# Feature blocks bank by bank at both ends of an output step, x blocks three ahead, two small moves

## The chip, the cores and the metric

The kernel runs on one core of one Trainium2 chip. The metric is device time in microseconds, the median of several runs. The core has five engines that work side by side, each with its own queue of instructions that it runs in order: PE (TensorE, matrix products into PSUM banks), PEld (its weight loads), DVE (VectorE), ACT (ScalarE), POOL (GpSimd), and SP, which here issues nearly all DMAs. They wait for each other by semaphores.

## The reference

One inference step of a decoder layer that mixes two branches. 1024 prompt tokens with 16 learned meta tokens ahead of them, and 8 x 4 sample tokens with a paged cache of 1024 positions, go through a common input projection, a stick-breaking attention branch and a gated linear attention branch, a gate on each, and one output projection:

```
h = rms_norm(x, norm_pre_g)
(q, k, v), sg, (gq, gk, gv, gf), gg = branch_inputs(h, w_in, w_alpha, b_alpha)
o_sb = sb_prompt(q, k, v, sb_bias)            # or sb_sample with the paged cache
o_gla, s_end = gla_prompt(gq, gk, gv, gf)     # or gla_chunk on the sample states
mixed = concatenate([o_sb * silu(sg), rms_norm(o_gla) * silu(gg)])
x = x + rms_norm(mixed @ w_out, norm_post_g)
```

Inside `branch_inputs`, the logarithm of the decay is `log_sigmoid(ga @ w_alpha + b_alpha) / 16`, with `ga` the 16 low-rank columns of the input projection. All is float32. The outputs are y for prompt and samples, the new keys and values, and the new states.

## The kernel before

Every float32 product is three products of a rounded high half and the remaining low half of its operands (high x high, high x low, low x high), so a matmul of the algorithm is three matmuls on PE.

The program is written as a main line of projections with side work woven in. A `Weaver` holds generators; `W.beat()`, called after every few matmuls, lets those that are due issue their next instructions. The order in each engine's queue is then set at build time by a planner that simulates the program: of the instructions that are ready in its simulation it takes the one written first, and those written under `urgent()` ahead of all others. It sets the semaphores too. `add_manual_dep(..., NOSYNC)` only forces an order in a queue.

Three stages matter here.

**Low-rank columns** (`low_rank`, lines 367 to 389). Three PSUM accumulators collect the 32 rows of `ga` (high and low weights) for three chunks of tokens. For each of five pieces ACT writes the rounded value to rows 0 to 31 of the tile `g` (L387) and again to rows 64 to 95 (L388), both from PSUM, and DVE writes the remainder to rows 32 to 63 (L389). The next input projection takes the same accumulators.

**Sample states** (`chunks`, lines 985 to 1053). For each of four GLA heads, after the eight prompt chunks, a loop over the eight samples b multiplies keys by values (L1042) and updates a state (L1044). States come by DMA into five buffers: those of b = 5, 6, 7 are loaded at the end of turns 0, 1, 2 (`load_state`, L993). The query products with the states (L1035) are issued in two groups of four, at b = 0 for states 0 to 3 and at b = 6 for states 4 to 7.

**Output projection** (lines 1288 to 1664). The product mixed @ w_out is done with seven products of half-size blocks, numbered p, in place of eight. Each p has two column halves q, and each (p, q) is a `step`: eight feature blocks k of 128 rows, four PSUM banks t of 128 tokens x 512 columns. For each k, `weights` asks for a 128 x 512 weight block by DMA into one of seven `wr` buffers (L1393), casts it on ACT into the high half (L1394) and subtracts on DVE for the low half (L1395), in a ring of four slots; then `product` issues three matmuls into each of the four banks (L1595 to L1597). The steps p = 1, 2, 3, 7 also have sixteen small sample products (L1615) after k = 3 and after k = 7, which read the raw weight blocks, so a `wr` buffer is free only after them. At the end of a step `take` copies or adds the four banks to SBUF (L1443, L1446, L1453, L1456, L1461, L1465, some urgent). Steps run in pairs (1,2), (6), (5,3), (7,4); the second of a pair adds into the same banks once the first's have been read, and the next pair takes two free banks and the first two of the last pair. The last step, (4, 1), has weights kept in SBUF and runs bank by bank throughout (lines 1656 to 1663).

Beside steps 7 and 4, `finish0` (L1510) finishes the first 512 tokens: sixteen blocks of x are fetched by DMA into the four `fr` buffers (L1519), DVE multiplies the output by its norm and adds x (L1530), and the result is stored (L1531). A fetch is ordered on SP behind the newest weight load that was written by then (`behind_ring`). For the first eight blocks a turn lasts two beats, for the others one.

Of the kernel before, what the change touches and what calls it, by code (L numbers as in the profile page):

```python
# [84 lines left out]
def hybrid_step(ctx: ExitStack, tc: tile.TileContext, x_prompt, x_sample, cache_k, cache_v, state_gla,  # L85
# [281 lines left out]
    def low_rank():  # L367

        acc = [accp.tile([P, 512], F32, tag="acc", name=f"acc_ga_{c}") for c in range(3)]
        for kb in range(0, NK, 4):  # L370
            for c, (lo, hi) in enumerate(CHUNKS):
                n = hi - lo
                for k in range(kb, kb + 4):
                    mm(acc[c][:32, :n], wa[k // 8][:, k % 8, :], hh[k][:, lo:hi], start=(k == 0), stop=False)
                    mm(acc[c][:32, :n], wa[k // 8][:, k % 8, :], hl[k][:, lo:hi], start=False, stop=(k == NK - 1))
                W.beat()
            W.beat()
        while not ga:
            W.beat()
        g = ga[0]  # L380
        for c, (lo, hi) in enumerate(CHUNKS):
            for a, b, d in ((max(lo, META), min(hi, REAL), -META), (lo, META, SEQ), (REAL, hi, 0)):
                if a >= b:
                    continue
                with urgent():
                    ps, cs = acc[c][:32, a - lo:b - lo], slice(a + d, b + d)
                    act.copy(g[0:32, cs], ps)  # L387
                    act.copy(g[64:96, cs], ps)  # L388
                    vec.tensor_tensor(g[32:64, cs], ps, g[0:32, cs].bitcast(F32), ALU.subtract)  # L389

    lvl = {}

# [344 lines left out]
    with tc.tile_pool(name="gp", bufs=1) as gp, tc.tile_pool(name="gps", bufs=1, space=PSUM) as gps:  # L737
# [247 lines left out]
        def chunks(g, at, qt, gv, pv, res):  # L985

            kd, ebl, pk = res["kd"], res["ebl"], res["pk"]
            S = None
            Ss = {}

            def load_state(b):
                Ss[b] = gp.tile([P, DV], F32, tag="Sb", bufs=5, name=f"Sb{g}_{b}")
                nc.sync.dma_start(Ss[b][:], state_gla[0, b, g])  # L993

            U = gps.tile([P, DV], F32, tag="U", name=f"U{g}_m")
            for f in range(2):
                mm(U[:, f * P:(f + 1) * P], kd[:META, 8 * P:9 * P], gv[f][:META, 8 * P:9 * P], start=True, stop=True)
            S = gp.tile([P, DV], F32, tag="S", bufs=2, name=f"S{g}_m")
            act.copy(S[:], U[:])
            yield 2  # L1000
            for c in range(8):
                ow = stage(f"ow{g}_{c}")
                ssq = gp.tile([P, 2], F32, tag="ssq", bufs=3, name=f"gssq{g}_{c}")
                U = gps.tile([P, DV], F32, tag="U", name=f"U{g}_{c}")
                for f in range(2):
                    mm(U[:, f * P:(f + 1) * P], kd[:, c * P:(c + 1) * P], gv[f][:, c * P:(c + 1) * P], start=True, stop=True)
                o = gps.tile([P, DV], F32, tag="o", name=f"o{g}_{c}")
                for f in range(2):
                    oh = o[:, f * P:(f + 1) * P]
                    mm(oh, at[:, slot(c), :], gv[f][:, c * P:(c + 1) * P], start=True, stop=False)  # L1010
                    mm(oh, qt[:, col(c):col(c) + P], S[:, f * P:(f + 1) * P], start=False, stop=True)
                Sn = gp.tile([P, DV], F32, tag="S", bufs=2, name=f"S{g}_{c}")
                vec.scalar_tensor_tensor(Sn[:], S[:], ebl[:, c:c + 1], U[:], ALU.mult, ALU.add)
                S = Sn
                act.copy(ow[:, :DV], o[:])
                act.activation(o[:], ow[:, :DV], AF.Square, accum_out=ssq[:, 0:1])
                W.spawn(chunk_out(g, c, ow, ssq[:, 0:1]), 1)
                if c > 2:
                    load_state(c - 3)
                yield 2  # L1020
            nc.sync.dma_start(new_state_prompt[0, 0, g], S[:])

            os_ = gps.tile([P, 2, DV], F32, tag="o", name=f"os{g}")
            for f in range(2):
                for i in range(2):
                    for j in range(4):
                        b = 4 * i + j
                        mm(os_[32 * j:32 * j + 32, i, f * P:(f + 1) * P], at[:48, 8, 16 + NT * b:48 + NT * b],
                           gv[f][:48, 8 * P:9 * P], start=(f == 0 and i == 0), stop=False, skip_group_check=True)
            for b in range(NB):  # L1030
                if b in (0, 6):
                    for j in range(4):
                        e = b // 6 * 4 + j
                        n = REAL + NT * e
                        mm(os_[32 * j:32 * j + 32, b // 6, :], qt[:, n:n + 32], Ss[e][:], start=False, stop=True,  # L1035
                           skip_group_check=True)
                Sb = Ss[b]
                km = stg.tile([96, 384], F32R, tag="stg", name=f"km{g}_{b}")[:, :P]
                vec.tensor_scalar(km, pk[:].bitcast(F32), rmask[:, b:b + 1], None, ALU.mult)
                yield 2  # L1040
                U = gps.tile([P, DV], F32, tag="U", name=f"Us{g}_{b}")
                mm(U[:], km, pv[:], start=True, stop=True)  # L1042
                sn = stage(f"sn{g}_{b}")[:, :DV]
                vec.scalar_tensor_tensor(sn, Sb[:], ebl[:, 9 + b:10 + b], U[:], ALU.mult, ALU.add)  # L1044
                nc.sync.dma_start(new_state_sample[0, b, g], sn)
                if b + 5 < NB:
                    load_state(b + 5)
            ssq = gp.tile([P, 2], F32, tag="ssq", bufs=3, name=f"gssq{g}_s")
            ow = [stage(f"ow{g}_s{i}")[:, :DV] for i in range(2)]
            for i in range(2):  # L1050
                act.copy(ow[i], os_[:, i, :])
                act.activation(os_[:, i, :], ow[i], AF.Square, accum_out=ssq[:, i:i + 1])
            W.spawn(samples_out(g, ow, ssq), 1)
# [236 lines left out]
    with ExitStack() as out:  # L1290
# [219 lines left out]
        def finish0():  # L1510
            r = scale((0, 1, 2, 3))
            todo = [(i, b) for i in range(4) for b in (0, 1)] + [(i, b) for i in range(4) for b in (2, 3)]
            xs = {}

            def fetch(n):
                if n < len(todo):
                    i, b = todo[n]
                    xs[n] = raw(f"xr{i}_{b}")[:]
                    behind_ring(nc.sync.dma_start(xs[n], x_prompt[0, i * P:(i + 1) * P, b * 512:(b + 1) * 512]).ins)  # L1519

            def load_xr(i, b):
                behind_ring(nc.sync.dma_start(xr[i, b], x_prompt[0, 512 + i * P:512 + (i + 1) * P, b * 512:(b + 1) * 512]).ins)

            fetch(0)
            fetch(1)
            for n, (i, b) in enumerate(todo):
                fetch(n + 2)
                yield 2 if n < 8 else 1
                o = sums_[i, b]
                vec.scalar_tensor_tensor(o, o, r[:, i:i + 1], xs.pop(n), ALU.mult, ALU.add)  # L1530
                nc.sync.dma_start(y_prompt[0, i * P:(i + 1) * P, b * 512:(b + 1) * 512], o)  # L1531
                if n == 7:
                    late_ = [slot(14 + f, f"xrs{f}") for f in range(2)]
                if n >= 8:
                    xr[i, b - 2] = late_[b - 2][:, i * 512:(i + 1) * 512].bitcast(F32)
                    load_xr(i, b - 2)
            for i in range(4):
                for b in (2, 3):
                    xr[i, b] = ytile(f"xr1_{i}_{b}")
                    load_xr(i, b)  # L1540
                    yield 1
# [59 lines left out]
        def step(p, q, banks, first, last):  # L1601
# [2 lines left out]
            if p in (1, 3):  # L1604
                SB[c, q] = ops.tile([P, 512], F32, tag="S", bufs=2, name=f"sc{c}{q}")
            raws = []
            for k in range(8):
                w = weights(p, q, k)
                for t in range(4):
                    product(banks[t], t, p, k, w[:2], first, last)  # L1610
                if c is not None:
                    raws.append(w[2])
                    if k % 4 == 3:
                        for e, j in itertools.product((k - 3, k - 1), range(4)):
                            mm(SB[c, q][32 * j:32 * j + 32, :256], small[SAMPLE[p]][:, e + j // 2, :],  # L1615
                               raws[e % 4 + j // 2][:, j % 2 * 256:j % 2 * 256 + 256], start=p in (1, 3) and e == 0,
                               stop=p in (2, 7) and e == 6, skip_group_check=True)
                        raws = []
                W.beat()
# [74 lines left out]
```

## Time and profile before

| | |
|---|---|
| runs | 2058.46, 2059.08, 2063.94 us |
| median | 2059.08 us |
| the profiled execution's own time | 2062.69 us |
| its span, first to last instruction | 2061.0 us |
| mean granted clock of PE | 0.998 |
| HBM read, written | 241.75 MB, 57.31 MB |
| output projection on PE | from 1718.0 us to 2051.4 us |

The profile is of one execution. Its page gives each engine's busy time; the view of waits says for which engine's instruction, or for which DMA, another stood idle, with total, times and longest. A timeline row has start, duration, engine, line, operation, output and inputs, shape, count, and in brackets the idle time before it and what ended it. Matmuls overlap, so the durations in the rows are longer than the distance from one to the next; the distance is what counts. Names such as `b` (output banks), `ring` (weight halves), `wr` (weight blocks), `q` (quarters of the mixed features), `xr` (x blocks), `u`, `y`, `c` (output sums) are those of the program.

### The profile page before, as it was taken

What the parts mean: (1) busy time and instruction counts of PE and PEld (TensorE: products, weight loads), DVE (VectorE), ACT (ScalarE), POOL (GpSimd) and SP (SyncE); (2) the same over time, 40 slices, a digit from 0 to 9 for tenths busy, and PEclk for the clock granted to TensorE, in tenths of its full rate; (3) what the DMA queues carried; (4) which work ended last, traced back from release to release, by engine and by line L of the source; (5) the groups of instructions that cost most, each with busy time, mean ns of one, the idle gap of its engine ahead of it and who ended that gap; (6) DMA issues with size and microseconds to landing.
All of it is one profiled execution on the core that took longest, in us unless ns stands there. A gap on an engine that the chain in (4) does not pass through costs nothing.

```text
span 2061.0 us, 41982 instructions
## 1 busy us (share of the span) xinstructions
PE 2023.1 (98%) x12507; PEld 1864.4 (90%) x12507; DVE 1551.5 (75%) x6282; ACT 953.5 (46%) x2293; POOL 85.1 (4%) x304
## 2 busy tenths in 40 slices
PE   6999999999999999999999999999999999999998
PEld 5999999999999998999999999999888898788776
DVE  7368989888988989899898888978444347554566
ACT  7355555565655556433534335343433325432332
POOL 0012000101000000000000000000000000000000
PEclk9999999999999999999999999999999999999999
DMA  6344454645455452443433434335776666352475
GB/s 202 104 139 147 140 158 134 169 134 147 146 157 147 141 126 73 138 107 80 108 103 80 126 81 115 93 87 166 241 228 230 222 227 195 134 163 75 148 272 175
DMA packets 371821, 301.85 MB, mean 146 GB/s; under 512 B 42360, under 2 KB 312104, under 8 KB 371592
## 3 DMA queue, kind: packets, MB, share of 16 engines
q1 hardware_dynamic: 371288, 298.64, 48.5%
q8 instruction: 98, 1.61, 0.3%
q14 instruction: 131, 1.07, 0.2%
q10 hardware_dynamic: 304, 0.53, 0.1%
HBM read 241.75 MB, written 57.31 MB: 145 GB/s over the span
## 4 chain that ended last, share of the span: by engine, by line
PE 84%; DVE 7%; DMA 3%; ACT 3%; issue 2%; SPq 1%; POOL 0%; DVEq 0%; ACTq 0%; POOLq 0%
PE acc_g L342 5%; PE acc_g L343 5%; PE acc_g L344 5%; PE b L1595 4%; PE b L1597 4%; PE b L1596 4%; PE acc_gv L342 3%; PE acc_gv L343 3%; PE acc_gv L344 3%; PE acc_k L342 3%; PE acc_k L344 3%; PE acc_k L343 3%; PE acc_v L342 2%; PE acc_v L344 2%; PE acc_v L343 2%; PE acc_q L342 2%
## 5 line engine op out<-in xcount | busy, mean ns | idle before, releaser
L464 DVE SCALAR_TENSOR_TENSOR jk<-kp,qb 128x128 f32<-128x128 f32 x2048 | 592.9, 289 | 43.2 <-DMA qb<-qsd 1.5
L342 PE MATMUL acc_g<-hT,wh_g 128*128 128x368 f32 (+2 forms) x768 | 251.1, 327 | 0.5 <-DVE ga L389 0.5
L343 PE MATMUL acc_g<-hT,wh_g 128*128 128x368 f32 (+2 forms) x768 | 247.2, 322 | 0.0
L344 PE MATMUL acc_g<-hT,wl_g 128*128 128x368 f32 (+2 forms) x768 | 246.8, 321 | 0.0
L1595 PE MATMUL b<-ring,f 128*128 128x512 f32 x416 | 164.7, 396 | 4.7 <-DVE u L1465 2.1
L464 DVE DVE_READ_ACCUMULATOR jk<-kp,qb 128x1 f32 x2048 | 166.7, 81 | 0.0
L1596 PE MATMUL b<-ring,f 128*128 128x512 f32 x416 | 163.3, 392 | 0.2 <-DVE ring L1395 0.2
L1597 PE MATMUL b<-ring,f 128*128 128x512 f32 x416 | 162.5, 391 | 0.0
L342 PEld LDWEIGHTS acc_g<-hT,wh_g 128*128 128x128 f32 x768 | 144.3, 188 | 13.1 <-issue 11.2
L1395 DVE TENSOR_TENSOR ring<-wr,ring 128x512 fp32r<-128x512 f32 x104 | 71.3, 689 | 102.4 <-ACT ring L1394 100.2
L343 PEld LDWEIGHTS acc_g<-hT,wh_g 128*128 128x128 f32 x768 | 144.4, 188 | 0.7
L344 PEld LDWEIGHTS acc_g<-hT,wl_g 128*128 128x128 f32 x768 | 144.2, 188 | 0.0
L1394 ACT CAST ring<-wr 128x512 fp32r<-128x512 f32 x104 | 64.2, 620 | 143.4 <-PE b L1597 83.7
L342 PE MATMUL acc_gv<-hT,wh_gv 128*128 128x400 f32 (+2 forms) x384 | 130.3, 339 | 0.0
L342 PE MATMUL acc_k<-hT,wh_k 128*128 128x384 f32 (+1 forms) x384 | 126.3, 329 | 0.0
L343 PE MATMUL acc_gv<-hT,wh_gv 128*128 128x400 f32 (+2 forms) x384 | 125.2, 326 | 0.0
L342 PE MATMUL acc_q<-hT,wh_q 128*128 128x368 f32 (+2 forms) x384 | 124.9, 325 | 0.0
L344 PE MATMUL acc_gv<-hT,wl_gv 128*128 128x400 f32 (+2 forms) x384 | 124.6, 325 | 0.0
L344 PE MATMUL acc_k<-hT,wl_k 128*128 128x384 f32 (+1 forms) x384 | 124.6, 324 | 0.0
L343 PE MATMUL acc_k<-hT,wh_k 128*128 128x384 f32 (+1 forms) x384 | 124.4, 324 | 0.0
L344 PE MATMUL acc_q<-hT,wl_q 128*128 128x368 f32 (+2 forms) x384 | 123.3, 321 | 0.0
L343 PE MATMUL acc_q<-hT,wh_q 128*128 128x368 f32 (+2 forms) x384 | 123.2, 321 | 0.0
(454 smaller groups left out, 5288.7 us busy)
## 6 DMA issues: line engine op xcount, KB each, us to landing
kp<-in_cache_k_dram SPq DMA_DIRECT2D x512, 64.0 KB
vr<-in_cache_v_dram SPq DMA_DIRECT2D x64, 512.0 KB
tf<-in_w_out_dram SPq DMA_DIRECT2D x64, 256.0 KB
td<-tf SPq DMA_DIRECT2D x64, 256.0 KB
qb<-qsd SPq DMA_DIRECT2D x64, 256.0 KB
wr_g<-in_w_in_dram SPq DMA_DIRECT2D x64, 256.0 KB
wr<-td SPq DMA_DIRECT2D x56, 256.0 KB
wr<-in_w_out_dram SPq DMA_DIRECT2D x48, 256.0 KB
```

The lines of the kernel that those rows point to most:

```text
L342: mm(acc[c][:, :n], wh, hh[k][:, lo:hi], start=(k == 0), stop=False)
L343: mm(acc[c][:, :n], wh, hl[k][:, lo:hi], start=False, stop=False)
L344: W.mark = mm(acc[c][:, :n], wl, hh[k][:, lo:hi], start=False, stop=(k == NK - 1)).ins
L464: ins = vec.scalar_tensor_tensor(jk[:], kp[:], 1.0, qbs[h, b][:, t, :], ALU.mult, ALU.mult, accum_out=zt[:, t, NPG - 1 - i:NPG - i])
L1394: act.copy(wh, r)
L1395: vec.tensor_tensor(wl, r, wh.bitcast(F32), ALU.subtract)
L1595: mm(bk[:], ah, wh, start=first and k == 0, stop=False, skip_group_check=True)
L1596: mm(bk[:], ah, wl, start=False, stop=False, skip_group_check=True)
L1597: mm(bk[:], al, wh, start=False, stop=last and k == 7, skip_group_check=True)
```

## The change

Four edits. In `low_rank` the five copies to rows 64 to 95 become one, from rows 0 to 31 in SBUF, after the loop and without urgency. In `chunks` the second group of query products is issued at b = 7 in place of 6. In `finish0` three x blocks are asked for at the start and then always three ahead, in place of two. In `step` the blocks k = 0, 1 and k = 6, 7 are taken as pairs: both weights are prepared first, and then each bank gets the products of both blocks before the next bank; the beat between them comes after the second bank.

```diff
@@ low_rank
                     ps, cs = acc[c][:32, a - lo:b - lo], slice(a + d, b + d)
                     act.copy(g[0:32, cs], ps)
-                    act.copy(g[64:96, cs], ps)
                     vec.tensor_tensor(g[32:64, cs], ps, g[0:32, cs].bitcast(F32), ALU.subtract)
+        act.copy(g[64:96, :], g[0:32, :].bitcast(F32))
@@ chunks
             for b in range(NB):
-                if b in (0, 6):
+                if b in (0, 7):
                     for j in range(4):
-                        e = b // 6 * 4 + j
+                        e = b // 7 * 4 + j
                         n = REAL + NT * e
-                        mm(os_[32 * j:32 * j + 32, b // 6, :], qt[:, n:n + 32], Ss[e][:], start=False, stop=True,
+                        mm(os_[32 * j:32 * j + 32, b // 7, :], qt[:, n:n + 32], Ss[e][:], start=False, stop=True,
                            skip_group_check=True)
@@ finish0
-            fetch(0)
-            fetch(1)
+            for n in range(3):
+                fetch(n)
             for n, (i, b) in enumerate(todo):
-                fetch(n + 2)
+                fetch(n + 3)
                 yield 2 if n < 8 else 1
@@ step
             raws = []
-            for k in range(8):
-                w = weights(p, q, k)
+            for ks in ((0, 1), (2,), (3,), (4,), (5,), (6, 7)):
+                k = ks[-1]
+                ws = [weights(p, q, i) for i in ks]
                 for t in range(4):
-                    product(banks[t], t, p, k, w[:2], first, last)
+                    for i, w in zip(ks, ws):
+                        product(banks[t], t, p, i, w[:2], first, last)
+                    if t == 1 and len(ks) == 2:
+                        W.beat()
                 if c is not None:
-                    raws.append(w[2])
+                    raws.extend(w[2] for w in ws)
                     if k % 4 == 3:
```

## Prediction

> **What bounds the kernel.** I read the page first, then the chain of waits and the waits of PE, then the windows around the longest of the late waits, and last the timelines of PE, ACT, DVE and the SP queue where the edits fall.
>
> ```profile
> span 2061.0 us, 41982 instructions
> ...
> PE 2023.1 (98%) x12507; PEld 1864.4 (90%) x12507; DVE 1551.5 (75%) x6282; ACT 953.5 (46%) x2293; POOL 85.1 (4%) x304
> ```
>
> PE is busy for 98% of the span. The change removes no matmul and adds none, so it can only win the places where PE stands still. The waits of PE name them (engine and line, whom it waited for, us in total, times, longest):
>
> ```profile
> PE b L1595 <- DVE u L1465: 2.1, 1, 2.1
> PE os L1035 <- DMA Sb<-in_state_gla_dram: 1.5, 1, 1.5
> PE b L1595 <- ACT u L1443: 1.5, 1, 1.5
> ...
> PE b L1595 <- DVE y L1461: 1.1, 1, 1.1
> ...
> PE acc_g L342 <- DVE ga L389: 0.5, 1, 0.5
> ...
> PE b L1596 <- DVE ring L1395: 0.2, 1, 0.2
> ```
>
> These six rows are everything the change can reach: 2.1 + 1.5 + 1.5 + 1.1 + 0.5 + 0.2 = 6.9 us, a third of a per cent of the span. The longest one costs more than it says. The windows view (stretch, its length, busy us and count of PE, PEld, DVE, ACT, POOL, then the granted clock) shows it:
>
> ```profile
> 2001.50:2004.90 3.40, 1.29 (x6) 0.73 (x5) 2.80 (x5) 0.81 (x3) 0.00 (x0) 1.00 1.05 399
> 2005.00:2008.40 3.40, 3.40 (x10) 2.62 (x9) 3.40 (x7) 2.68 (x8) 0.00 (x0) 0.50 0.91 305
> 2008.40:2011.80 3.40, 3.40 (x17) 2.80 (x16) 3.40 (x6) 0.62 (x1) 0.00 (x0) 1.00 0.53 183
> ```
>
> In the stretch of the wait PE works 1.29 us of 3.40, and in the next one the clock is 0.50. Half of 3.4 us, 1.7 us, is lost there on top. Reachable in all: 6.9 + 1.7 = 8.6 us.
>
> **The output steps, gain.** A step is 96 matmuls, twelve for each feature block k (three into each of four banks), and two sets of sample products where there are any.
>
> ```profile
> 1736.33 0.39 PE L1595 MATMUL b<-ring,f 128*128 128x512 f32 x1
> ...
> 1738.42 0.51 PE L1595 MATMUL b<-ring,f 128*128 128x512 f32 x1
> 1739.14 0.50 PE L1596 MATMUL b<-ring,f 128*128 128x512 f32 x1 [0.22 <-DVE ring L1395]
> ...
> 1741.88 1.07 PE L1615 MATMUL sc<-wr,small 128*32 128x256 f32 x16
> 1744.42 0.50 PE L1595 MATMUL b<-ring,f 128*128 128x512 f32 x1 [1.47 <-ACT u L1443]
> ```
>
> From 1736.33 (k=6, second bank) to 1738.42 (k=7, first bank) nine matmuls start, 0.23 us each. Today a bank's last matmul ends nine matmuls, 2.05 us, before its first of the next step; with the last two and the first two blocks bank by bank it is eighteen, 4.1 us. The two banks that the next pair takes from the last one come due twelve matmuls after the start, not six: 1.4 us later. The order adds no work: the same 96 matmuls at the same pitch, with six in a row into a bank instead of three.
>
> For the waits on L1465 (start of step 7, second half) and L1461 (start of step 4), the rows of the SP queue, DVE and PE:
>
> ```profile
> 1969.03 0.42 SPq L1519 DMA_DIRECT2D xr<-in_x_prompt_dram  x1
> ...
> 1974.98 0.75 DVE L1530 SCALAR_TENSOR_TENSOR c<-c,vrt_y,xr 128x512 f32<-128x512 f32 x1 [3.49 <-DMA xr<-in_x_prompt_dram]
> ...
> 1977.56 2.48 DVE L1461 TENSOR_TENSOR y<-b,y 128x512 f32<-128x512 f32 x4
> ...
> 2002.10 0.75 DVE L1530 SCALAR_TENSOR_TENSOR y<-y,vrt_y,xr 128x512 f32<-128x512 f32 x1 [1.60 <-DMA xr<-in_x_prompt_dram]
> ...
> 2003.37 1.88 DVE L1465 TENSOR_TENSOR u<-b,u 128x512 f32<-128x512 f32 x3
> ...
> 2004.11 0.51 PE L1595 MATMUL b<-ring,f 128*128 128x512 f32 x1 [2.11 <-DVE u L1465]
> ```
>
> DVE runs its queue in order, and both evacuations stand behind an L1530 that waits for its x block. So two edits help: banks are free earlier and due later, and the block comes earlier. Asked for three ahead, a block is asked for one turn (two beats of twelve matmuls, 5.5 us; one beat, 2.7 us, in the second half) sooner, if a buffer is free. There are four buffers, and four blocks are then held, so a fetch waits for the L1530 before it; the store issued next waits for that one as well, so SP is blocked no longer than now. SP issues the same sixteen loads, only earlier. At 2004.11 alone the later due time covers 1.4 of the 2.1 us, and an x block 0.7 us earlier covers the rest. I take the 2.1 + 1.7 and the 1.1 us as gone. Bounds: nothing of the 1.1 and 1.4 of the 2.1 at the least, all 4.9 at the most.
>
> **The output steps, price.** The weights of k=1 and k=7 come due nine matmuls, 2.05 us, sooner: straight after three matmuls of their neighbour. A ring slot of k=0 or k=6 comes free 2.05 us later. In steps with sample products, k=7 has the least time, because its buffer is one that the sample products after k=3 release. Two cases of it, the first in step 1, the second in the step 1 that follows:
>
> ```profile
> 1731.74 0.32 SPq L1298 DMA_DIRECT2D q<-md  x1
> 1732.11 2.38 SPq L1393 DMA_DIRECT2D wr<-in_w_out_dram  x3
> ...
> 1737.74 1.38 ACT L1394 CAST ring<-wr 128x512 fp32r<-128x512 f32 x2
> ...
> 1743.79 2.04 ACT L1443 COPY u<-b 128x512 f32<-128x512 f32 x4
> ```
>
> ```profile
> 1780.51 2.20 SPq L1393 DMA_DIRECT2D wr<-in_w_out_dram  x4
> ...
> 1783.60 0.62 ACT L1394 CAST ring<-wr 128x512 fp32r<-128x512 f32 x1 [2.51 <-DMA wr<-in_w_out_dram]
> ...
> 1784.25 0.69 DVE L1395 TENSOR_TENSOR ring<-wr,ring 128x512 fp32r<-128x512 f32 x1 [2.36 <-ACT ring L1394]
> ...
> 1789.17 0.39 PE L1595 MATMUL b<-ring,f 128*128 128x512 f32 x1
> ```
>
> In the quiet case the load takes 3.1 us (1780.51 to 1783.60), the low half is ready at 1784.94, and PE wants it at 1789.40: 4.5 us of room, 2.4 after the change. In the first case the load stands behind q<-md on SP, takes 5.6 us, and the cast ends at 1738.36, just when k=7 begins at 1738.42. After the change k=7 is due at 1736.33. PE, with everything behind it in its queue, waits 2.09 us for the high half, and its second matmul starts at 1739.14 instead of 1738.65, 0.49 more: 2.6 us. Then the sample products end at about 1745.2. By then L1443 (from 1743.79) has copied the first bank, so the waits of 1.5 and 0.2 us are gone, yet 2.6 us stand in their place. ACT is late there by a q block of its own, which this change does not touch. Bounds for the new wait: nothing, if the load lands in the 3.1 us of the quiet case (1735.2, both halves by 1736.6, when the second matmul is due); 2.6 + 1.7 = 4.3 if the clock halves after it. I take 2.6, the nearest row.
>
> [...]
>
> **Sample outputs and low-rank copies.**
>
> ```profile
> 1408.19 0.62 PE L1035 MATMUL os<-Sb,gq 128*32 128x256 f32 x2 [1.55 <-DMA Sb<-in_state_gla_dram]
> 1409.78 0.28 PE L1042 MATMUL Us<-pv,km 96*128 96x256 f32 x1
> ```
>
> The last two products wait for state 7. Moved behind the U product of b=6 (1409.78 now, 1408.2 without the wait), they find it landed at 1408.1. Gain 1.5 us, bounds 0 and 1.5; the later release of qt and the os bank is covered by the next group's key projection. The other three groups did not wait.
>
> ```profile
> 783.18 0.53 ACT L388 CAST ga<-acc_ga 32x384 fp32r<-32x384 f32 x2
> ...
> 783.68 0.63 DVE L389 TENSOR_TENSOR ga<-acc_ga,ga 32x384 fp32r<-32x384 f32 x2 [0.35 <-ACT ga L388]
> ```
>
> L389 waits for L388, which read the same bank and no longer stands there. The accumulator is free about 0.5 us earlier, so the 0.5 us goes (bounds 0 and 0.5). The one copy of 1072 columns that replaces the five casts is an estimate of 1.0 to 1.5 us from this row, on an ACT that is 46% busy, and nothing reads it for tens of us; if it stood ahead of an urgent cast, it could cost up to that.
>
> **Sum.** Removed 8.6, added 2.6: 6.0 us. The profiled execution took 2062.69 us, span and 1.7 us around it, so 2056.7. The other runs were 2058.46, 2059.08 and 2063.94. The profiled one belongs to the upper pair, some 4 us above the lower. I read the 3.8 us of the 2004 gap as the difference, since it hangs on when a DMA lands. Then the median of 2059.08 has only 4.8 us to lose, and 2059.1 - 4.8 + 2.6 = 2056.9, the same place. If the median run had the gap too, it is 2059.1 - 6.0 = 2053.1. Forecast **2056.7**, own range 2053 to 2060. A difference under 0.3% (6.2 us) can hardly be told from none.
>
> **Rivals.**
> 1. The new wait fails to appear and the median run held every stall: 2059.1 - 8.6 = 2050.5. For it: the quiet load has 2.4 us left. Against it: SP's order before 1732.11, and the spread of the runs. Chance 0.24.
> 2. The x blocks stay late, because SP sets them behind the weights as at 1969.03, and DVE stays late: 1.1 us and 0.7 of the 2.1 remain, 2056.7 + 1.8 = 2058.5. Chance 0.18.
> 3. The half clock stays: it comes after the new wait of 2.1 + 0.5 us, or was never due to the gap: 2056.7 + 1.7 = 2058.4. Chance 0.10.
> 4. Slower: the k=7 load is late in every step with sample products. Seven steps besides the first have some 2 us left after the change; a load of 3.1 us decides for none, one above about 5.5 us decides for all. At 6.6 us, 3.5 more than the quiet row, each waits about 1.5 us: 2056.7 + 7 x 1.5 = 2067.2. The 5.6 us of the first step and the 5.9 us of the x block at 1969.03 speak for it, the quiet steps against it. Chance 0.08.
>
> That leaves 0.40 for the forecast. Faster by over 0.3%: rival 1 and the low edge of the forecast, 0.27. Slower: rival 4, 0.08. Within: 0.65. The range of 2049.5 to 2062 holds the forecast and the first three rivals and leaves out the fourth and the edges.
>
> **What would show it.** Right: no PE wait on L1465, L1461, L1443, L389 or Sb, and a PE wait of 2 to 3 us on the ring in the first step. L1530 waits less than now for xr. Wrong: ring waits in later steps, a bank wait that survives, or waits of PE in the stages between, whose order the planner may set anew.

## The result, and the profile after

The changed kernel takes 2065.64 us (median of 6 runs, 2064.95 to 2067.73), the kernel before 2058.77 us in the same comparison (6 runs, 2056.00 to 2063.94). The ratio is 1.0031, with a 95% interval of 1.0021 to 1.0041: slower by about 7 us, where 2056.7 was forecast. The profiled execution took 2064.97 us.

The page of the changed kernel begins like this:

```profile
span 2063.3 us, 41971 instructions
...
PE 2023.3 (98%) x12507; PEld 1863.9 (90%) x12507; DVE 1553.9 (75%) x6282; ACT 953.5 (46%) x2289; POOL 85.2 (4%) x304
```

PE's work is the same, to the matmul, and its busy time is within 0.2 us of before. The difference is in how long it stands idle. These are the rows of PE's waits that answer to the six of before:

```profile
PE b L1596 <- DVE ring L1395: 4.9, 6, 1.7
...
PE b L1595 <- ACT ring L1394: 2.2, 3, 1.0
...
PE os L1035 <- DMA Sb<-in_state_gla_dram: 1.8, 1, 1.8
...
PE acc_g L342 <- ACT gx L521: 0.2, 1, 0.2
```

The waits on L1465, L1443, L1461 and L389 are gone, as forecast. The wait for the state `Sb` is still there. New are 7.1 us of waiting for the halves in the ring, 4.9 for the low ones and 2.2 for the high ones, where before had 0.2.

The half clock has moved as well. The windows around the `Sb` wait (the column after POOL is the granted clock):

```profile
1403.00:1406.40 3.40, 1.64 (x13) 0.70 (x12) 2.18 (x11) 0.62 (x1) 0.00 (x0) 1.00 0.98 325
1406.40:1409.80 3.40, 3.40 (x12) 3.22 (x12) 1.40 (x8) 1.76 (x6) 0.00 (x0) 0.50 0.47 143
1409.80:1413.20 3.40, 3.40 (x23) 3.40 (x22) 2.38 (x15) 0.38 (x2) 0.00 (x0) 1.00 0.18 58
```

In the middle row the clock is 0.50 and PE makes 12 matmuls where the next makes 23: again half of 3.4 us, 1.7 us, is lost. So the two profiled executions can be set against each other. Before had 6.9 us in the six waits and 1.7 us of half clock, 8.6. After has 7.1 + 1.8 + 0.2 and 1.7, 10.8. PE's other waits, in the stages that the change doesn't touch, add up to 20.6 us before and 20.4 after. The difference of the rows is 2.2 us, and the spans differ by 2.3. The profiled execution of before was one of its long ones, 3.9 us above its median; that of after lies 0.7 us below its median. The three together, 2.3 + 3.9 + 0.7, are the 6.9 us between the medians.

Where the ring waits begin is seen at the start of step (2, 0), the first that they hit. Timelines of PE, ACT and DVE of the changed kernel:

```profile
1741.22 0.39 PE L1597 MATMUL b<-ring,f 128*128 128x512 f32 x1
...
1742.22 1.07 PE L1619 MATMUL sc<-wr,small 128*32 128x256 f32 x16
1743.22 0.50 PE L1595 MATMUL b<-ring,f 128*128 128x512 f32 x1
...
1744.09 0.50 PE L1595 MATMUL b<-ring,f 128*128 128x512 f32 x1
1746.29 0.50 PE L1596 MATMUL b<-ring,f 128*128 128x512 f32 x1 [1.70 <-DVE ring L1395]
```

```profile
1742.44 1.07 ACT L1443 COPY u<-b 128x512 f32<-128x512 f32 x2
1743.40 0.64 ACT L1394 CAST ring<-wr 128x512 fp32r<-128x512 f32 x1
```

```profile
1743.18 1.29 DVE L1354 TENSOR_TENSOR q<-q,s 128x512 f32<-128x512 f32 x2
1744.94 0.69 DVE L1354 TENSOR_TENSOR q<-q,s 128x512 f32<-128x512 f32 x1 [0.47 <-DMA q<-md]
1745.55 0.69 DVE L1395 TENSOR_TENSOR ring<-wr,ring 128x512 fp32r<-128x512 f32 x1
```

The bank is free in time here: k=0 starts at 1743.22, straight after the sample products. Three matmuls later, at 1744.09, PE is at k=1. Its high half has just been cast (1743.40), behind the copies of the banks, and its low half (1745.55 and 0.69 us) ends at 1746.24, behind two DVE groups of other work. PE waits 1.70 us for it. Read one by one, the ring waits of the changed kernel are 1.2 us at k=7 of step (1, 0), the one that was forecast, 0.1 at k=7 of step (7, 0), and 5.9 us at **k=1**: 1.7 and 0.6 in steps (2, 0) and (2, 1), 0.3 in (7, 0), 1.8 in (4, 0) and 1.5 in (7, 1).

Why k=1 is late in just these steps is in the code around the change. A weight takes the ring slot `j = next(turn) % 4` (L1382). But `gain`, called before each step that evacuates with a norm factor, draws its name from the same counter:

```python
            t = op.tile([P, 512], F32, tag="gpost", bufs=2, name=f"gpost{b}_{next(turn)}")
```

So in the steps (2, ·), (3, ·), (7, ·) and (4, 0) the slots are shifted by one, in both kernels: k=0 gets the slot of the previous step's k=5 and k=1 that of its **k=6**. In the old order k=6 ends 12 matmuls before the end of its step and k=1 is due 12 after the start of the next: 24 matmuls at 0.23 us, 5.5 us. With both pairs bank by bank, k=6 ends 3 before the end and k=1 is due 3 after the start: 6 matmuls, 1.4 us, and 1.0 us of sample products. In that time the cast (0.64 us) and the subtraction (0.69 us) have to fit, and they stand in queues with the evacuations of the step that has just ended. With one pair alone it would be 15 matmuls, 3.4 us.

The short distance alone doesn't make the wait. In steps (3, ·) the slots are shifted too, and no sample products widen the 1.4 us, yet PE has no ring wait there. ACT, DVE and PE of the changed kernel at the start of (3, 0):

```profile
1884.10 1.30 ACT L1394 CAST ring<-wr 128x512 fp32r<-128x512 f32 x2 [4.14 <-PE b L1597]
```

```profile
1884.76 0.69 DVE L1395 TENSOR_TENSOR ring<-wr,ring 128x512 fp32r<-128x512 f32 x1 [0.65 <-ACT ring L1394]
```

```profile
1885.51 0.50 PE L1596 MATMUL b<-ring,f 128*128 128x512 f32 x1
```

ACT stands idle until PE has let go of the slot, and DVE until the cast is done. The first cast of the group is k=1's; its low half ends at 1885.45, 0.06 us before PE comes to it. In (2, 0) the last product of k=6 starts at 1741.22 and takes 0.39 us, so the slot is free at 1741.61, but the cast starts only at 1743.40 and the subtraction at 1745.55. So it takes both: the slot that comes free late holds the cast back to the end of the step, and there the evacuations and the work on the mixed features stand ahead of it.

### The profile page after: what moved, and what is told of

It reads as the page before. It is cut to its first block, busy times and chain, and to the rows that moved or that the text cites. A ratio compares the mean times of both kernels' runs of the same rounds, so it can differ in the third digit from the quotient of the medians.

```text
span 2063.3 us, 41971 instructions
## 1 busy us (share of the span) xinstructions
PE 2023.3 (98%) x12507; PEld 1863.9 (90%) x12507; DVE 1553.9 (75%) x6282; ACT 953.5 (46%) x2289; POOL 85.2 (4%) x304
## 4 chain that ended last, share of the span: by engine, by line
PE 83%; DVE 7%; DMA 4%; ACT 2%; issue 2%; SPq 1%; POOL 0%; DVEq 0%; ACTq 0%; POOLq 0%
PE acc_g L342 5%; PE acc_g L343 5%; PE acc_g L344 5%; PE b L1596 4%; PE b L1595 4%; PE b L1597 4%; PE acc_gv L342 3%; PE acc_gv L343 3%; PE acc_gv L344 3%; PE acc_k L342 3%; PE acc_k L344 3%; PE acc_k L343 3%; PE acc_v L342 2%; PE acc_q L342 2%; PE acc_q L344 2%; PE acc_q L343 2%
## 5 line engine op out<-in xcount | busy, mean ns | idle before, releaser
L342 PE MATMUL acc_g<-hT,wh_g 128*128 128x368 f32 (+2 forms) x768 | 251.6, 328 | 0.2 <-ACT gx L521 0.2
L342 PEld LDWEIGHTS acc_g<-hT,wh_g 128*128 128x128 f32 x768 | 144.9, 189 | 12.5 <-issue 10.8
L1394 ACT CAST ring<-wr 128x512 fp32r<-128x512 f32 x104 | 64.0, 621 | 146.0 <-PE b L1597 79.2
L342 PE MATMUL acc_gv<-hT,wh_gv 128*128 128x400 f32 (+2 forms) x384 | 130.3, 339 | 0.0
L342 PE MATMUL acc_k<-hT,wh_k 128*128 128x384 f32 (+1 forms) x384 | 126.3, 329 | 0.0
L342 PE MATMUL acc_q<-hT,wh_q 128*128 128x368 f32 (+2 forms) x384 | 124.9, 325 | 0.0
```

The lines of the kernel that those rows point to most:

```text
L342: mm(acc[c][:, :n], wh, hh[k][:, lo:hi], start=(k == 0), stop=False)
L1394: act.copy(wh, r)
```

## The experiments

Eleven runs of ten kernels in three groups; the kernels of a group share the runs of the kernel before (2060.66 us, 2060.06 us and 2059.63 us in the median of 29, 33 and 21 runs).

| kernel | median us (runs) | ratio to before, 95% interval | ring waits of PE, us |
|---|---|---|---|
| after, old step order | 2060.27 (11) | 0.9999, 0.9990 to 1.0009 | none |
| before, new step order | 2068.13 (6) | 1.0041, 1.0027 to 1.0055 | 7.3 |
| after, last pair only | 2062.91 (11) | 1.0011, 1.0001 to 1.0021 | 4.1 |
| after, first pair only | 2056.97 (11) | 0.9984, 0.9975 to 0.9993 | 0.6 |
| after, own counter | 2056.90 (11) | 0.9989, 0.9980 to 0.9998 | 2.2 |
| before, own counter | 2061.47 (11) | 1.0009, 1.0000 to 1.0018 | none |
| own counter, states forced | 2055.39 (11) | 0.9980, 0.9970 to 0.9989 | 2.9 |
| own counter, x two ahead | 2057.59 (11) | 0.9989, 0.9980 to 0.9998 | 3.6 |
| first pair, own counter, states forced | 2053.57 (11) | 0.9972, 0.9963 to 0.9981 | 0.9 |
| after, gain takes two numbers | 2067.43 (5) | 1.0037, 1.0023 to 1.0050 | 10.1 |
| own counter, states forced, again | 2055.77 (11) | 0.9981, 0.9972 to 0.9990 | 3.0 |

The ring waits are those of the one execution of each kernel that was profiled. It took 2059.04 us with the last pair only, 3.9 below the median, and 2061.98 with x two ahead and 2071.50 with two numbers, 4.4 and 4.1 above it. So rows and medians of these three don't belong to the same execution.

**Which edit costs.** The first kernel undoes the step order and keeps the other three edits; the second does the step order alone.

```diff
-            for ks in ((0, 1), (2,), (3,), (4,), (5,), (6, 7)):
+            for k in range(8):
...
```

> The changed kernel with the old order of feature blocks in the steps; x blocks three ahead, late sample products and the single low-rank copy stay. Theory A (the slowdown is the order in the steps: k=1 and k=7 come due before their weight halves are ready): the ring waits of PE, 7.1 us in the changed kernel, fall under 1 us, some bank waits on L1443 and L1461 come back (1 to 3 us), time 2057 to 2060, about that of the kernel before. Theory B (the slowdown comes from the other three edits or from the planner setting the stages between anew, and from the half clock after the wait for state 7): time stays at 2064 to 2066.

> The kernel before with the new order in the steps alone. Theory A: ring waits of PE of 6 to 8 us, no bank waits, time 2064 to 2066, slower than before by 5 to 8 us. Theory B: the ring waits replace the bank waits one for one and the time is that of the kernel before, 2057 to 2060.

With the old order the time is that of before, 2060.27 us, and no ring wait is left. PE's waits of that kernel:

```profile
PE os L1035 <- DMA Sb<-in_state_gla_dram: 1.9, 1, 1.9
PE b L1595 <- ACT u L1443: 1.4, 1, 1.4
PE b L1595 <- DVE u L1465: 1.1, 1, 1.1
...
PE acc_g L342 <- ACT gx L521: 0.8, 1, 0.8
```

The bank waits are back instead, 2.5 us. The step order alone costs all of it, 2068.13 us, and it has 5.3 + 2.0 us of ring waits. So the cause is in the step order, and the other three edits together are worth a few microseconds at most.

**Which pair.** Only the last two blocks, or only the first two, bank by bank:

```diff
-            for ks in ((0, 1), (2,), (3,), (4,), (5,), (6, 7)):
+            for ks in ((0,), (1,), (2,), (3,), (4,), (5,), (6, 7)):
```

> The changed kernel with only the last two blocks (6, 7) as a pair; k=0 and k=1 one by one as before. Theory A with the price at k=1 (its weights stand behind the evacuation of the last step on ACT and DVE, and it is due after three matmuls): the waits at k=1, about 5 us of the 7, go; banks are still free 4.1 us before their next use at the first bank, 2.7 us at the last, so no bank wait; time 2058 to 2060, 5 to 7 us under the changed kernel. Theory with the price at k=7 (a load that starts only after the sample products): waits stay, 2063 to 2066.

> The changed kernel with only the first two blocks (0, 1) as a pair; k=6 and k=7 one by one. Price at k=1: waits at k=1 stay or grow, since the evacuations end later, time 2064 to 2067. Price at k=7: only the wait of 1.2 us at k=7 in the first step and 0.1 at step 7 go, 2063 to 2065 by that reading too unless k=1 frees itself; a time under 2061 would say that k=7 carried the cost.

The last pair alone gives 2062.91 us, above the 2058 to 2060 that I had set for a price at k=1 and just below the 2063 to 2066 for k=7. Its eleven runs fall into four of 2058.4 to 2059.3 and seven of 2061.8 to 2066.1, and the profile is of one of the four; what makes the seven longer is not known. The first pair alone gives 2056.97. With the last pair alone no wait at k=1 of (2, 0), (2, 1) or (4, 0) is left; its ring waits are the one at k=7 of (1, 0), 1.3 us, and two in step (7, 1), 1.8 us at k=0 and 1.0 at k=1. The DVE timeline of that kernel shows where the two come from:

```profile
1996.48 0.75 DVE L1530 SCALAR_TENSOR_TENSOR y<-y,vrt_y,xr 128x512 f32<-128x512 f32 x1 [3.41 <-DMA xr<-in_x_prompt_dram]
1997.15 0.68 DVE L1395 TENSOR_TENSOR ring<-wr,ring 128x512 fp32r<-128x512 f32 x1
```

The subtraction for k=0 stands behind an L1530 that waits 3.41 us for its x block, and PE waits 1.80 us for it at 1997.88. The evacuations behind it run later by as much, and the subtraction for k=1 behind those. An x block that held banks before holds the ring here. By its ratio this kernel has a good third of the cost of both pairs (1.0011, against 0.9999 for the old order and 1.0031 for both). The first pair alone has none of it: its only ring wait is 0.6 us at k=1 of (4, 0), and of the bank waits the one on L1443 is back with 1.4 us. By my expectation, which set k=1 against k=7, its time spoke for k=7. But k=7 waits 1.3 us with the last pair alone and 1.2 with both, and the waits at k=1 of step (2, ·) are there only with both. Each pair by itself is innocent of those; it takes the two, as the distances of 6, 15 and 24 matmuls between two users of a slot would have it.

**The slot.** `gain` gets a counter of its own, in the changed kernel and in the one before:

```diff
-        turn = itertools.count()
+        turn, gained = itertools.count(), itertools.count()
...
-name=f"gpost{b}_{next(turn)}")
+name=f"gpost{b}_{next(gained)}")
```

> The changed kernel, with a counter of its own for the name of the gain tile. In the kernels so far `gain` takes a number from the counter that also picks the ring slot, so after a gain k=1 of a step gets the slot of k=6 of the step before, not that of k=5. Slot theory: with both pairs, k=6 lets go of its slot three matmuls before the step ends and k=1 is due three matmuls into the next, 1.4 us (2.4 with the sample products) for a cast and a subtraction of 1.3 us and whatever stands before them; with its own counter k=1 has 27 matmuls, 6.1 us. The waits at k=1 (5.9 us of the 7.1 in the changed kernel) go, those at k=7 (1.2 in the first step) stay; time 2058 to 2061 where the kernel before has 2060.7, 5 to 7 us under the changed kernel. Queue theory (k=1 is late only because ACT and DVE do the evacuations first): the evacuations are as early as in the changed kernel, waits at k=1 stay over 3 us, time within 2 us of the changed kernel.

> The kernel before with the counter of its own alone. Slot theory: there k=6 lets go twelve matmuls before the end and k=1 is due twelve after, so the slot costs nothing: the bank waits on L1443, L1461 and L1465 stay as they fall, no ring wait, time that of the kernel before within 0.1%. If the time falls by more than 0.15%, the shifted slots cost something before the change too.

One number in a name is worth 8.7 us to the changed kernel (2065.64 to 2056.90, ratios of 1.0031 and 0.9989, each against its own runs of before) and brings nothing to the old order (ratio 1.0009, 1.0000 to 1.0018). In the changed kernel the waits at k=1 are gone; what is left is 1.6 us at k=7 of (1, 0) and 0.6 at k=2 of (7, 1). The row that was at 1744.09 and 1746.29 reads, in PE's timeline of this kernel:

```profile
1742.56 0.50 PE L1595 MATMUL b<-ring,f 128*128 128x512 f32 x1
...
1743.38 0.40 PE L1595 MATMUL b<-ring,f 128*128 128x512 f32 x1
1743.61 0.40 PE L1596 MATMUL b<-ring,f 128*128 128x512 f32 x1
```

and in ACT's the cast for k=1 is now the second of the group

```profile
1736.38 1.29 ACT L1394 CAST ring<-wr 128x512 fp32r<-128x512 f32 x2 [0.39 <-DMA wr<-in_w_out_dram]
```

which runs some six microseconds earlier than the 1743.40 of after, as soon as the weight has landed, since it takes the slot of k=5, which PE is done with before k=6.

**A larger dose.** Each gain takes two numbers, so that k=0 gets the slot of k=6 and k=1 that of k=7:

```diff
-name=f"gpost{b}_{next(turn)}")
+name=f"gpost{b}_{next(turn) + 0 * next(turn)}")
```

> The changed kernel, except that each gain takes two numbers of the slots' counter in place of one. Slot theory: after a gain k=0 gets the slot of k=6 and k=1 that of k=7, which with the two pairs are read until 3 and 0 matmuls before the step's end. The distance for k=1 falls from 6 matmuls (1.4 us) to 3 (0.7 us), and k=0 has 3 (0.7 us) too, against the 1.3 us that cast and subtraction take. The ring waits of PE in steps (2,0) to (4,0) grow from 6 us to at least 10, and the time is 2070 us or more. Rival (the seven us come from the order in which SP and ACT are loaded by the pairs, whatever the slot): ring waits stay at 5 to 8 us, and the time within 2 us of the changed kernel's 2065.6.

```profile
PE b L1595 <- ACT ring L1394: 6.2, 5, 2.2
PE b L1596 <- DVE ring L1395: 3.9, 6, 1.3
```

The waits grow to 10.1 us, and k=0 now waits too: its high half 0.42 and its low half 1.14 us in step (2, 0). The time, 2067.43 us, is 1.8 us above the changed kernel's, not the 4.4 or more that I had expected, and inside the 2 us that I had given to the rival. The profile speaks for the slot, the time alone doesn't decide. I had priced the dose as if it fell on every shifted step in full.

**The state products.** From the profile after: PE's timeline around them.

```profile
1403.59 0.63 PE L1035 MATMUL os<-Sb,gq 128*32 128x256 f32 x6
1405.98 0.68 PE L1035 MATMUL os<-Sb,gq 128*32 128x256 f32 x2 [1.76 <-DMA Sb<-in_state_gla_dram]
...
1407.06 0.41 PE L1042 MATMUL Us<-pv,km 96*128 96x256 f32 x1
```

The products were moved to b = 7 in the program, behind the U product of b = 6. In PE's queue they still stand ahead of it: the planner sets the order by its own simulation. The next kernel forces the order in the queue, on top of the own counter:

```diff
+                last = mm(U[:], km, pv[:], start=True, stop=True).ins
+                if b == 7:
+                    for j in range(4):
...
+                        tc.add_manual_dep(ins, last.name, NOSYNC, reason="behind")
```

> e5_own_counter, and the last four products with the states ordered on PE behind the U product of the last turn. Planner theory (the edit moved them in the program, but the planner issued them ahead of the U product of b=6 all the same, since its simulation had the state landed): the PE wait on Sb, 1.8 us, and the half clock after it in some executions go; 1.5 to 3.5 us under e5_own_counter. Rival: the wait moves to another engine's work (the copy of os or the states' update) and the time is that of e5_own_counter within 1 us.

In its profile the eight products stand behind the last U product and wait for nothing:

```profile
1406.95 0.39 PE L1042 MATMUL Us<-pv,km 96*128 96x256 f32 x1
1407.27 0.64 PE L1046 MATMUL os<-Sb,gq 128*32 128x256 f32 x8
```

No row of PE's waits names `Sb` any more. The median falls from 2056.90 to 2055.39, but the intervals of the two overlap, and the profiled execution is no shorter (span 2055.1 us against 2054.8): in it the wait at k=7 of (1, 0) is 2.6 us, with half clock behind it (0.51 from 1736.30 to 1739.70). So it is shown that the wait went, and not that the time fell by 1.5 us.

**The third x block.** The own counter, with x asked for two ahead as before:

```diff
-            for n in range(3):
-                fetch(n)
+            fetch(0)
+            fetch(1)
...
-                fetch(n + 3)
+                fetch(n + 2)
```

> e5_own_counter with x blocks asked for two ahead again. If the third block ahead carries part of the gain: DVE waits on L1530 for xr grow to over 8 us, a bank wait on L1465 or L1461 of 0.5 to 1.5 us returns, 1 to 3 us slower. If the banks' later due time alone covers the late blocks: no bank wait, time within 1 us of e5_own_counter.

DVE's waits for x in before, in after, and in this kernel:

```profile
DVE y L1530 <- DMA xr<-in_x_prompt_dram: 6.0, 3, 3.7
DVE c L1530 <- DMA xr<-in_x_prompt_dram: 5.6, 2, 3.5
```

```profile
DVE y L1530 <- DMA xr<-in_x_prompt_dram: 5.4, 4, 2.1
DVE c L1530 <- DMA xr<-in_x_prompt_dram: 2.7, 2, 2.4
```

```profile
DVE y L1530 <- DMA xr<-in_x_prompt_dram: 7.3, 2, 4.4
DVE c L1530 <- DMA xr<-in_x_prompt_dram: 1.8, 3, 0.9
```

With three ahead DVE waits 8.1 us in all (8.3 with the own counter), with two 11.6 and 9.1. No bank wait comes back with two: the later due time of the banks covers it alone in this profile. One 2.1 us ring wait appears in step (7, 1), again behind an L1530. The median is 0.7 us above that with three, which the intervals don't tell from nothing.

**The best of the parts.** First pair only, own counter, states forced; and, on the same chip, both pairs with the other two once more.

> Only the first pair of blocks, a counter of its own for gain, and the last four products with the states forced behind the last turn's U product. Slot theory: no ring wait at k=1 of any step and none at k=7 of step (1,0), since the last pair is gone; no wait for Sb; what is left of PE's waits in the output steps is at most the 1.4 us at L1443 and some x wait, so 2053 to 2056 us, the fastest of all. Rival (the last pair is worth more than its wait at k=7, because it frees the next pair's banks): the bank waits at L1443 and L1465 come back with 1.4 and 1.1 us, and the time is that of the kernel with both pairs and the forced products, 2055 us, or above it.

> The kernel with both pairs, a counter of its own and the forced products once more, beside the one with the first pair alone. Slot theory: 2055 us again, 0 to 2 us above the first pair alone, the difference being the wait at k=7 of step (1,0). Rival (last pair worth more than that wait): at or below the first pair alone.

2053.57 us and 2055.77 us. The first is the fastest kernel of the study, 6 us below before. PE's waits in its output steps (its lines are six further down, so L1449 is L1443 and L1400 is L1394):

```profile
PE b L1601 <- ACT u L1449: 1.1, 1, 1.1
...
PE b L1601 <- ACT ring L1400: 0.7, 1, 0.7
...
PE b L1602 <- DVE ring L1401: 0.2, 1, 0.2
```

I had expected no wait at k=7 of (1, 0) without the last pair, and there are 0.9 us of it. So that wait isn't the pair's alone: in before the cast was ready with 0.06 us to spare, behind an ACT cast of a q block that had waited 2.75 us for its DMA. What held it in this kernel is not shown. Of the bank waits, the one on L1443 is back with 1.1 us and the one on L1465 is not. The 2.2 us between the two kernels agree with the last pair being worth less than its price, but their intervals overlap (0.9963 to 0.9981 and 0.9972 to 0.9990), and the wait at k=7 of (1, 0) accounts for 0.5 of them by the profiles (1.4 against 0.9).

## Why the prediction was wrong

**What bounds the kernel.** Right: PE's stalls are what this change acts on, and the stalls added up for each kernel give the difference of the two spans within 0.1 us. The rows of before say nothing of what it can add.

**Gains in the output steps.** Right in mechanism: the bank waits of 2.1, 1.5 and 1.1 us and the 1.7 us of half clock behind the first went, and the old order brings 2.5 us of them back. The third x block was not needed for that: with the pairs, two blocks ahead leave no bank wait either. In one profile of both pairs (own counter, states forced, again) 0.3 us of bank wait at the start of step (4, 0) is left.

**The price of the step order.** This is the step that failed. The prediction says that "the weights of k=1 and k=7 come due nine matmuls, 2.05 us, sooner" and that "a ring slot of k=0 or k=6 comes free 2.05 us later", and then bounds k=7 alone, because "k=7 has the least time". The room of k=1 was never read, so it was priced at nothing. It cost 5.9 us in the profile. The row was there. In before's DVE and PE timelines at the same place:

```profile
1744.17 0.69 DVE L1395 TENSOR_TENSOR ring<-wr,ring 128x512 fp32r<-128x512 f32 x1
```

```profile
1747.52 0.39 PE L1596 MATMUL b<-ring,f 128*128 128x512 f32 x1
```

The low half of k=1 is ready at 1744.86 and PE wants it at 1747.52: 2.7 us of room, from which 2.05 are taken by the order and 1.5 more by the bank wait that goes. That alone is a wait of 0.9 us, an estimate; 1.7 was measured. The two sentences were also never joined: a slot that comes free 2.05 us later and a user that comes 2.05 us sooner is one distance, shorter by 4.1 us, as soon as one knows which k takes over which slot. I took it that k=1 follows k=5. The line that says otherwise is L1423, which takes a number of the slots' counter.

**k=7 of the first step.** Mechanism right, size too large: forecast 2.6 us, measured 1.2 in after (0.2 to 2.6 in the other profiles with the last pair, 0.9 at most without it). With states forced it is 2.6 and the half clock follows (0.51 over 3.40 us), the upper bound of 4.3; the bounds were right, and where in them a run falls was luck. The fourth rival, whose 2067.2 us is near the result, isn't what happened: it had k=7 late in every step with sample products because of its load. Of those, k=7 waits 0.1 us in one.

**State products.** Wrong. "Moved behind the U product" was true of the program and not of the queue. It cost 1.8 us for 1.5, and in the profiled execution a half clock of 1.7 us with it. Forced in the queue, the wait is gone; the gain in time isn't clear of the noise.

**Low-rank copies.** The 0.5 us that PE waited on L389 went, and the one copy took 1.09 us on ACT with nobody waiting for it (estimate 1.0 to 1.5). In after (0.2 us) and in the kernel with the old steps (0.8) L342 waits on ACT's L521 instead; the step order alone, without this edit, has that row too (0.6), so it isn't shown to be the price of this edit.

**The sum.** Forecast: 8.6 removed, 2.6 added. By the profiles: 7.1 removed (all but the `Sb` wait), and 9.4 added, namely 5.9 at k=1, 1.3 at k=7, 1.7 of half clock at 1406, and 0.5 in small rows. With k=1 and the state products corrected, 2062.69 - 7.1 + 9.4 is 2065.0, the profiled 2064.97. What it came to agree with is the two profiled executions; the reading that the median run of before lacks the 3.8 us of the gap at 2004 fits the difference between profile and median, but it was not seen in a profile of such a run and stays argued.

## What to carry to other kernels

When an order is changed so that one user of a buffer ends later and the next begins sooner, write down which instance takes over from which, for every step, before any price is put on it: the distance between the two is the room, and it shrinks at both ends at once. A rotating index that something else also advances, here by a name, makes that table differ from step to step, and an old order with 24 matmuls of room (5.5 us here) hides it. Then look at what stands ahead in the queues at that moment: here six matmuls of room, 1.4 us, were just enough where nothing did (0.06 us left in step (3, 0)). And a move in the program is a move in the queue only where the planner is made to keep it: read it from the timeline, not from the diff.

## What the chip did that was not expected

The half clock doesn't follow from the length of a gap. In the kernel where gain takes two numbers, PE stands 2.24 us, from 1986.48 to 1988.72, and the granted clock stays at 1.00:

```profile
1983.87:1987.28 3.41, 2.61 (x24) 1.41 (x22) 3.41 (x7) 1.86 (x5) 0.00 (x0) 1.00 0.75 211
1987.28:1990.69 3.41, 1.97 (x8) 1.23 (x8) 3.26 (x7) 3.38 (x9) 0.00 (x0) 1.00 1.05 295
1990.69:1994.11 3.42, 3.42 (x16) 2.85 (x16) 3.36 (x7) 0.59 (x3) 0.00 (x0) 1.00 1.01 350
```

In the kernel with x two ahead, a gap of 1.31 us and one of 0.23 right behind it are followed by the half clock:

```profile
1736.42 0.49 PE L1595 MATMUL b<-ring,f 128*128 128x512 f32 x1 [1.31 <-ACT ring L1394]
```

```profile
1734.67:1738.08 3.41, 1.87 (x7) 1.01 (x7) 2.08 (x3) 2.02 (x4) 0.00 (x0) 1.00 0.96 307
1738.08:1741.49 3.41, 3.41 (x10) 2.63 (x9) 2.59 (x4) 2.04 (x4) 0.00 (x0) 0.50 0.88 337
```

The loss was half of 3.4 us wherever it was read: the clock is 0.50 for 3.41 us in before (from 2004.96), in after (from 1406.41) and with x two ahead (from 1738.08). In before and in after the clock is halved once more behind a window in which PE did nothing, from 2056.16 and from 2058.36, which is 51.20 and 651.95 us after the first time: 15 and 191 lengths of 3.413 us.

What sorts most of the cases is where a gap falls between marks that lie such lengths apart, counted from a half clock of the same trace. Cut at them, before has 2.11 us of idle PE in the window that ends at 2004.96, and after has 1.76 us in the one that ends at 1406.41. No other window of these two traces between 20 and 2040 us has more than 1.70, and none of the others is followed by half clock. The wait for `Sb` shows both sides: in after its 1.76 us lie in one window; in before a mark at 1407.63 splits the 1.55 us into windows with 0.99 and 0.56 idle, and the clock stays at 1.00. The windows of this section are cut in the same way. With two numbers the half clock begins at about 1407.03, an estimate from the clocks of 0.74 in 1405.40:1408.80 and 0.76 in 1408.80:1412.20. The mark at 1987.28, 170 lengths later, splits the 2.24 us into 0.80 and 1.44; with x two ahead the 1.31 and the 0.23 us fall into one window, 1.54. But the idle time in a window doesn't sort all of them: 1.54 was followed by half clock, and 1.70 (the wait that ends at 1746.29 in after) was not.

So a gap of one to two microseconds has, in this kernel, a price of itself or of itself and 1.7 us, and one profile can't tell which of the two the median run pays.
